# Scores of the second query half: two 64-row tiles with half of the keys each, three products in place of four

## The chip, the core and the metric

The kernel runs on one core of one Trainium2 chip. The metric is the device time of one execution in microseconds (us). Engines are named as in the profile: PE is TensorE (matrix products), PEld its weight loads, DVE is VectorE, ACT is ScalarE, POOL is GpSimd, SP is SyncE, which issues the DMA transfers.

## What is computed

One layer over 1024 tokens with a model width of 1024, in float32: an input projection, two kinds of attention with 8 heads of 64 columns each, an output projection, a sandwich norm and a gated per-layer embedding. The change concerns the scores z of both attentions:

```python
def stick_breaking_attention(q, k, v):          # "SB", strictly causal
    z = jnp.einsum('bqhd,bkhd->bhqk', q_blk, k).astype(jnp.float32) * scale
    past = key_idx[None, :] < t_idx[:, None]
    log_fail = jnp.where(past, jax.nn.log_sigmoid(-z), 0.0)
    suffix = lax.cumsum(log_fail, axis=3, reverse=True) - log_fail
    w = jnp.where(past, jnp.exp(jax.nn.log_sigmoid(z) + suffix), 0.0)

def latent_attention(q_nope, q_rope, k_nope, k_rope, v):   # "MLA"
    z = (jnp.einsum('bqhd,bkhd->bhqk', qn, k_nope)
         + jnp.einsum('bqhr,bkr->bhqk', qr, k_rope)).astype(jnp.float32) * scale
    visible = key_chunk[None, :] <= q_chunk[:, None]       # chunks of 64 tokens
    w = jax.nn.softmax(jnp.where(visible, z, -jnp.inf), axis=-1)
```

In SB and in the first MLA term 64 rows are contracted, in the rotary term (`qr`) 32.

## The kernel before

Every float32 operand of a product is split into a high part and a low part (type float32r), whose sum is the value, and stored so. A product of two values is then up to four products of parts: high x high, high x low, low x high, low x low.

**Units.** Attention goes by units (head c, e; query half s): `SEQ` (line 60) lists the order of the pairs of heads, c below 4 for SB and from 4 on for MLA, e for the head in the pair, s = 0 or 1 for the first or second 512 queries. A unit has four query blocks of 128 (`qi`); block qi of half s sees nk = (4s + qi + 1) x 128 keys. So in the second half nk is 640, 768, 896 or 1024, handled as two parts of h = 320, 384, 448 or 512 keys (`score_tiles`, line 1255), the first half of the keys and the second, each in a PSUM bank of its own.

**Scores.** `load_head` (line 1227) stacks the operands of a unit on all 128 partitions. The key tile `kk` has the 64 rows of a head twice, high and low in alternation; `qa` has the query rows as (high, low), `qb` as (low, high), read from `q_d` forwards and backwards. Two products of 128 contracted rows, qa x kk and qb x kk, so make all four products of parts. `sb_rows` (line 1263) issues them for each part of the keys, and for the part with the diagonal a bf16 product `eye` x `mask` that puts -1e30 on what isn't past; ScalarE then takes two sigmoids from the bank. `mla_rows` (line 1295) has a third product, the rotary one: `qr` x `krs`, 128 rows too (32 rows x high and low of each side). VectorE sets the hidden corner to -1e30, takes the maximum, and ScalarE the exponential. That is 4 products per block of the second half in SB, 6 in MLA. After that come transposes of the weights and the products with the values (`av`, line 1325).

**Order.** Nothing is issued as written. A recorder (lines 340 to 760, `R`) collects all instructions with their operands, estimates a duration for each (`cost`), and `schedule` lays them out engine by engine in a simulation of its own. Each takes its turn by its place in the program, moved by the table `SHIFT` (line 70), which has two numbers for each piece of the program; `FLIP` has the numbers of instructions that change between VectorE and GpSimd or ScalarE. Scores go out 52 places early (`AHEAD`). Other work (projections, gates, norms) is woven in between by `Weaver`, so score products stand among products of other parts. All instructions are issued from one line, 730, so the profile is read by tiles: `t` and `a` are PSUM banks (5 and 3 of them), `u` and `f` buffers in SBUF, `h` larger ones. Loads of a unit are issued a unit ahead (`prepare`).

Of the kernel before, what the change touches and what calls it, by code (L numbers as in the profile page):

```python
# [15 lines left out]
BF16 = mybir.dt.bfloat16  # L16
# [19 lines left out]
MAGIC = 12582912.0  # L36
PI_LO = 3.1415925
# [10 lines left out]
def f(ap):  # L48
# [284 lines left out]
class Recorder:  # L333
# [116 lines left out]
    def columns(self, op, args):  # L450

        return self.elems(args[0]) * (2 if op == "transpose" else 1 if args[1].dtype in (F32R, BF16) else 4)

    @staticmethod
    def elems(ap):
        n = 1
# [4 lines left out]
    def cost(self, eng, op, args, kw, outs, aps, spaces):  # L461
        n = max(self.elems(a) for a in aps)
        ps = any(k == "psum" for _, k in spaces)
        if eng == "PE":
            n = self.elems(outs[0])
            if op == "transpose":
                return 109.0
# [1320 lines left out]
```

## Time and profile before

| | |
|---|---|
| three runs | 773.84, 775.03, 775.43 us |
| the profiled execution | 774.4 us, its span 772.6 us |
| share of the span: DMA queue q1 | 57.4% of 16 engines |
| loads of q_d, k_d in units, issue to landing | 4.7 us (256 KB), 5.3 us (512 KB) |
| table loads on ACT | 18 of 1.28 us |

The page has busy times by engine, the chain of work that ended last, and groups of instructions (operation, output <- inputs, shapes, count, busy us, mean ns of one, idle before). A matmul's end is modelled and overlaps with the next one's start, so the distance from start to start is what a product costs, not its duration. The slices of the page (40 of 19.3 us each) show TensorE's clock and VectorE:

```profile
DVE  5876334499867877788888899999899998888996
...
PEclk9999999999999999999999999999999999999999
```

TensorE has its full clock throughout; VectorE is busiest in the second half of the span.

### The profile page before, as it was taken

The numbers are of one execution on the slowest core, as the hardware profiler recorded it, in microseconds if no ns is written. First come the engines' busy times: TensorE is split into PE (matmuls) and PEld (weight loads), VectorE is DVE, ScalarE is ACT, GpSimd is POOL, SyncE is SP. The second block draws the span as 40 slices with busy tenths as digits, with TensorE's granted clock in tenths as the row PEclk, the third lists the DMA queues.
The fourth block names the chain that finished last, engine by engine and source line by source line (L and its number), as shares of the span: only waits on it lengthen the run. The fifth ranks groups of instructions, "written<-read, shape, count | busy, mean of one in ns | idle before, by whom it ended". The sixth has DMA issues, their size and how long they took to land.

```text
span 772.6 us, 11778 instructions
## 1 busy us (share of the span) xinstructions
PE 754.5 (98%) x3912; PEld 621.5 (80%) x3912; DVE 624.1 (81%) x1184; ACT 384.9 (50%) x898; POOL 346.6 (45%) x315
## 2 busy tenths in 40 slices
PE   6999999999999999999999899999999999999997
PEld 4887889878788878888788788888888888778886
DVE  5876334499867877788888899999899998888996
ACT  6315123333443586565646768776776642433211
POOL 4445111102312258878884712342275114468664
PEclk9999999999999999999999999999999999999999
DMA  9644460269995844566356588686734475172242
GB/s 329 201 171 139 145 213 5 77 218 354 330 341 190 275 155 143 167 206 189 110 184 225 187 290 260 216 302 223 240 116 154 166 254 178 60 268 87 94 150 82
DMA packets 101966, 148.69 MB, mean 192 GB/s; under 512 B 7441, under 2 KB 55057, under 8 KB 101906
## 3 DMA queue, kind: packets, MB, share of 16 engines
q1 hardware_dynamic: 101906, 147.95, 57.4%
q8 instruction: 31, 0.51, 0.3%
q14 instruction: 29, 0.24, 0.1%
HBM read 101.26 MB, written 46.66 MB: 191 GB/s over the span
## 4 chain that ended last, share of the span: by engine, by line
PE 84%; DVE 7%; DMA 4%; ACT 2%; issue 1%; POOL 1%; SPq 1%; POOLq 0%; ACTq 0%; DVEq 0%
PE a L730 58%; PE t L730 26%; DVE u L730 4%; DVE f L730 2%; ACT u L730 1%; DMA u<-k_d 1%; DMA u<-in_w_ple_gate_dram 1%; DMA u<-q_d 1%; DMA u<-in_x_dram 1%; DMA f<-in_positions_dram 1%; DMA q_d<-f 1%; SPq L730 1%; DVE nm L730 1%; ACT f L730 0%; POOL u L730 0%
## 5 line engine op out<-in xcount | busy, mean ns | idle before, releaser
L730 POOL TENSOR_TENSOR u<-u,u 128x512 f32<-128x512 f32 (+16 forms) x134 | 200.5, 1512 | 153.3 <-DVE u L730 64.0
L730 PE MATMUL a<-h,f 128*128 128x512 f32 x864 | 242.1, 405 | 0.0
L730 PEld LDWEIGHTS a<-h,f 128*128 128x128 f32 x864 | 155.2, 189 | 26.8 <-DVE f L730 0.6
L730 DVE TENSOR_TENSOR u<-t,u 128x512 fp32r<-128x512 f32 (+4 forms) x284 | 150.6, 556 | 13.7 <-ACT u L730 10.0
L730 PE MATMUL t<-u,u 128*128 128x512 f32 (+4 forms) x580 | 154.4, 370 | 1.9 <-DMA u<-q_d 0.5
L730 PE MATMUL a<-u,u 128*128 128x512 f32 (+2 forms) x524 | 136.7, 371 | 0.5 <-DVE u L730 0.5
L730 PE MATMUL t<-ident,u 128*128 128x128 f32 x792 | 125.8, 276 | 2.4 <-DVE u L730 2.4
L730 ACT ACTIVATE u<-t 128x512 f32<-128x512 f32 (+5 forms) x208 | 91.0, 509 | 67.7 <-PE t L730 57.8
L730 PEld LDWEIGHTS t<-u,u 128*128 128x128 f32 x580 | 103.4, 189 | 23.2 <-DVE u L730 4.3
L730 ACT CAST u<-t 128x512 fp32r<-128x512 f32 (+3 forms) x187 | 85.6, 495 | 71.0 <-PE t L730 35.3
L730 PE MATMUL a<-h,u 128*128 128x512 f32 (+1 forms) x492 | 118.3, 390 | 0.4 <-DVE u L730 0.4
L730 PEld LDWEIGHTS t<-ident,u 128*128 128x128 f32 x792 | 97.8, 142 | 24.9 <-DVE u L730 7.0
L730 PEld LDWEIGHTS a<-h,u 128*128 128x128 f32 x492 | 90.0, 188 | 21.3 <-issue 1.0
L730 PEld LDWEIGHTS a<-u,u 128*128 128x128 f32 x524 | 93.1, 188 | 17.2 <-DVE u L730 2.2
L730 ACT ACTIVATE u<-t,nms 128x384 f32<-128x384 f32 (+4 forms) x96 | 55.3, 581 | 42.3 <-DVE nms L730 35.3
L730 DVE TENSOR_TENSOR_SCAN u<-u 128x64 f32<-128x64 f32 (+6 forms) x64 | 59.1, 934 | 20.6 <-ACT u L730 20.4
L730 DVE TENSOR_TENSOR u<-u,u 128x512 f32<-128x512 f32 (+13 forms) x91 | 73.2, 820 | 2.0 <-ACT u L730 1.1
L730 DVE TENSOR_TENSOR u<-a,u 64x512 f32<-64x512 f32 (+4 forms) x75 | 47.8, 649 | 15.6 <-ACT u L730 9.7
L730 DVE TENSOR_REDUCE nm<-t 128x1 f32<-128x384 f32 (+4 forms) x96 | 51.6, 545 | 2.1 <-PE t L730 1.3
L730 POOL TENSOR_TENSOR rs<-ms,nhalf 128x8 f32<-128x8 f32 x16 | 27.7, 1731 | 57.0 <-DVE ms L730 37.5
L730 ACT ACTIVATE f<-a 128x512 bf16<-128x512 f32 (+3 forms) x64 | 34.3, 538 | 36.7 <-PE a L730 32.1
L730 PE MATMUL a<-u,h 128*128 128x512 f32 x192 | 49.8, 406 | 0.0
(110 smaller groups left out, 795.5 us busy)
## 6 DMA issues: line engine op xcount, KB each, us to landing
u<-q_d SPq DMA_DIRECT2D x64, 256.0 KB, 4.7
u<-k_d SPq DMA_DIRECT2D x16, 512.0 KB, 5.3
u<-v_d SPq DMA_DIRECT2D x16, 512.0 KB, 4.5
u<-in_w_ple_gate_dram SPq DMA_DIRECT2D x16, 512.0 KB, 5.4
f<-in_w_in_dram SPq DMA_DIRECT2D x14, 512.0 KB, 5.0
v_d<-u SPq DMA_DIRECT2D x12, 512.0 KB, 4.1
f<-in_x_dram SPq DMA_DIRECT2D x9, 512.0 KB, 4.6
k_d<-u SPq DMA_DIRECT2D x9, 512.0 KB, 3.9
```

The source lines that it names most:

```text
L730: x["fn"](*[place(a) for a in x["args"]], **{k: place(a) for k, a in x["kw"].items()})
```

## The change

The first query half (s = 0) keeps two stacked products, with another layout of the keys. In the second half (s = 1) a product contracts 64 rows instead of 128: a 64-row tile on partitions 0 to 63 and another on 64 to 127. Both hold the same queries; the lower has the keys of all even chunks of 64, the upper those of all odd chunks, so each tile has h = nk / 2 keys and writes a bank of its own. Per tile there are three products for SB and for the first term of MLA (`PARTS`: high x high, high x low, low x high; low x low is left out), and two for the rotary term, whose 64 rows are 32 rows of queries with high and low, against the high and the low keys. A block so has 3 pairs of products in SB and 5 in MLA. The diagonal mask becomes a pair too: `step` (64 rows each) x `diag` on the last 64 columns of both banks.

The keys are stored by halves (even chunks, odd chunks) for that; what is read from the banks goes back to its place in the row through a pattern of runs of 64. The planner counts an upper product at 5 ns, gets other costs for bf16 products and waits on DMA, and takes two engines that read one bank as one after the other; `SHIFT` and `FLIP` have other numbers throughout (left out below, as are the planner's lines on banks).

```diff
+PARTS = ((0, 0), (0, 1), (1, 0))
 def columns(self, op, args):
+        if self.upper(args[1]):
+            return 0
+    def upper(self, ap):
+        return ap.shape[0] == 64 and int(ap.offset) >= 64 * self.tiles[ap.tensor.name]["width"]
 def cost(self, eng, op, args, kw, outs, aps, spaces):
+            if self.upper(args[1]):
+                return 5.0
...
-                return n * 0.305
+                return n * 0.416
 LAT:
-("SP", "PE"): 650.0,
+("SP", "PE"): 950.0,
...
+    step, diag = const([128, 128], "step", BF16), const([128, 64], "diag", BF16)
-    k_d = [dram([128, 2, S], f"k_d{i}") for i in range(8)]
+    k_d = [dram([128, 2, 2, S // 2], f"k_d{i}") for i in range(8)]
+    def by_half(ap):
+        return ap.rearrange("q (b a d) -> q a b d", a=2, d=64)
+    def k_evac(dst):
+        def evac(ps, n):
+            t = k4((128, 2, 2, 4, 64), name="qkhl")
+            split(t[:, 0], t[:, 1], by_half(ps), heng=ACT)
+            SP.dma_start(dst[:, :, :, 256 * n:256 * n + 256], f(t.rearrange("q a h b d -> q a h (b d)")))
 def load_head(i, s):
+        if s == 0:
...
+            t = k2((128, 2, 256), name="stk")
+            SP.dma_start(f(t), k_d[c][rows, :, :, 0:256].rearrange("q a h n -> (q a) h n"))
+        else:
+            t = k4((128, 2, 512), name="stq")
+            src = q_d[c][rows, :, half[1]]
+            SP.dma_start(f(t), bass.AP(tensor=src.tensor, offset=src.offset, ap=[[0, 2], *src.ap]))
+            st.append(t)
+            t = k4((128, 2, 512), name="stk")
+            SP.dma_start(f(t), k_d[c][rows].rearrange("q a h n -> h q a n"))
...
+    def scores(s, qi, terms, masked):
+        nk = (4 * s + qi + 1) * 128
+        qc = slice(qi * 128, (qi + 1) * 128)
+        R.bias = -AHEAD
+        if s == 0:
+            ps, w = ps_s(), max(nk, 256)
+            for j, (q, k) in enumerate(terms):
+                mm(ps[:, 0:w], q[:, qc], in_order(k)[:, 0:w // 128], start=(j == 0), stop=(j == len(terms) - 1))
+                if masked and j == 0:
+                    mm(ps[:, nk - 128:nk], eye, mask, start=False, stop=False)
+            return nk, [(ps[:, 0:nk], lambda t: t[:, 0:nk])]
+        h = nk // 2
+        pss = [ps_s() for _ in range(2)]
+        for j, (q, k) in enumerate(terms):
+            for a, ps in enumerate(pss):
+                p = slice(64 * a, 64 * a + 64)
+                mm(ps[:, 0:h], q[p, qc], k[p, 0:h], start=(j == 0), stop=(j == len(terms) - 1),
+                   **({} if a or j else dict(along=pss[1])))
+            if masked and j == 0:
+                for a, ps in enumerate(pss):
+                    p = slice(64 * a, 64 * a + 64)
+                    mm(ps[:, h - 64:h], step[p], diag[p], start=False, stop=False)
+        see = lambda a: lambda t: by_half(t[:, 0:nk])[:, a]
+        return nk, [(ps[:, 0:h], see(a)) for a, ps in enumerate(pss)]
 def sb_rows(i, s, rows):
-            tiles, w = score_tiles(nk)
...
-                mm(ps[:, 0:w], qa[:, qc], kk[:, kw], start=True, stop=False)
-                if ks.stop == nk:
-                    mm(ps[:, h - 128:h], eye, mask, start=False, stop=False)
-                mm(ps[:, 0:w], qb[:, qc], kk[:, kw], start=False, stop=True)
+            nk, tiles = scores(s, qi, terms, True)
 def mla_rows(i, s, rows, es, e):
+            terms = [(st[0][:, a], st[1][:, b]) for a, b in PARTS] + [(st[2], krs[:, b]) for b in range(2)]
-                mm(ps[:, 0:w], qa[:, qc], kk[:, kw], start=True, stop=False)
-                mm(ps[:, 0:w], qb[:, qc], kk[:, kw], start=False, stop=False)
-                mm(ps[:, 0:w], qr[:, qc], krs[:, kw], start=False, stop=True)
+            nk, tiles = scores(s, qi, terms, False)
```

What that does to the order, in rows (output <- moving operand, stationary operand; the numbers name buffers). First TensorE at the first block of the first SB unit of the second half, before. `u_2510` holds the keys, `u_1709` and `u_1949` are qa and qb, `t_184` and `t_157` the two banks:

```order
L730 MATMUL t_184<-u_2510,u_1709 128x320
L730 MATMUL t_184<-u_2510,u_1949 128x320
L730 MATMUL t_157<-u_2510,u_1709 128x320
L730 LDWEIGHTS eye
L730 MATMUL t_157<-mask,eye 128x128
L730 MATMUL t_157<-u_2510,u_1949 128x320
```

The same block after the change; `u_2542` has the keys, `u_2512` the queries, `t_158` is written by the lower tile and `t_225` by the upper:

```order
L748 MATMUL t_158<-u_2542,u_2512 128x320
L748 MATMUL t_225<-u_2542,u_2512 128x320
L748 LDWEIGHTS step
L748 MATMUL t_158<-diag,step 128x64
L748 LDWEIGHTS step
L748 MATMUL t_225<-diag,step 128x64
L748 MATMUL t_158<-u_2542,u_2512 128x320
L748 MATMUL t_225<-u_2542,u_2512 128x320
```

A third pair like the last two rows follows. Four products of full height and one mask have become three pairs of half height and a pair of masks. Pairs stand together in most places, not in all. TensorE at the third block of the next unit after the change (`a_190` is the bank of the value products, of full height):

```order
L748 MATMUL t_218<-u_2739,u_2685 128x448
L748 MATMUL t_291<-u_2739,u_2685 128x448
L748 MATMUL a_190<-u_2074,u_2606 128x512
L748 MATMUL a_190<-u_1881,u_2606 128x512
L748 MATMUL a_190<-u_1905,u_2606 128x512
L748 MATMUL a_190<-u_1024,u_2606 128x512
L748 MATMUL a_190<-u_1853,u_2606 128x512
L748 MATMUL a_190<-u_1917,u_2606 128x512
L748 MATMUL t_218<-u_2739,u_2685 128x448
```

Six full-height products stand between the last product of `t_291` and its partner in `t_218`. In one block of an MLA unit the order has all five products of one tile ahead of the other's (`u_5273` and `u_4377` are the keys and the rotary keys):

```order
L748 MATMUL t_169<-u_5273,u_5268 128x384 x3
L748 MATMUL t_169<-u_4377,u_5261 128x384 x2
L748 MATMUL t_218<-u_5273,u_5268 128x384 x3
L748 MATMUL t_218<-u_4377,u_5261 128x384 x2
L748 MATMUL t_291<-ident,u_5308 128x128
```

Only the two in the middle are neighbours there. Counted over the whole order, the 576 products of half height form 71 stretches with nothing of full height inside.

More of the change, by code (lines that the diff above doesn't have):

```diff
@@ L431, in add @@
                 uses.append(key)
+        if along is not None:
+            self.tiles[along.tensor.name]["users"].append(i)
+            uses.append(along.tensor.name)
         dur = self.cost(eng, op, args, kw, outs, aps, spaces)
         reads = sum(a.shape[-1] > 1 and k == "sbuf" for a, (w, k) in zip(aps[1:], spaces))
+        banks = [a.tensor.name for a, (w, k) in zip(aps[1:], spaces) if k == "psum"]
         port = eng == "POOL" and op != "memset" or eng == "DVE" and (
@@ L513 @@
            ("DVE", "POOL"): 156.0, ("DVE", "SP"): 120.0, ("POOL", "PE"): 180.0, ("POOL", "ACT"): 75.0,
-           ("POOL", "DVE"): 65.0, ("POOL", "POOL"): 102.0, ("POOL", "SP"): 55.0, ("SP", "PE"): 650.0,
-           ("SP", "ACT"): 620.0, ("SP", "DVE"): 620.0, ("SP", "POOL"): 650.0, ("SP", "SP"): 620.0}
+           ("POOL", "DVE"): 65.0, ("POOL", "POOL"): 102.0, ("POOL", "SP"): 55.0, ("SP", "PE"): 950.0,
+           ("SP", "ACT"): 900.0, ("SP", "DVE"): 900.0, ("SP", "POOL"): 950.0, ("SP", "SP"): 900.0}
     def schedule(self):
@@ L553, in schedule @@
         table = None
+        read = {}
         clock = {}
@@ L668, in schedule @@
                     table = x["func"]
+                for key in x["banks"]:
+                    for y, t in read.get(key, {}).items():
+                        if y != e:
+                            s = max(s, t + LAT[y, e])
                 if x["port"]:
@@ L674, in schedule @@
                 free[e] = end
+                for key in x["banks"]:
+                    read.setdefault(key, {})[e] = end
             done += 1
@@ L789, in block_kernel @@
     DVE.tensor_copy(eye, ident)
+    step, diag = const([128, 128], "step", BF16), const([128, 64], "diag", BF16)
+    POOL.memset(step, 1.0)
+    POOL.affine_select(step, step, pattern=[[-1, 128]], compare_op=ALU.is_ge, fill=0.0,
+                       base=0, channel_multiplier=1)
+    DVE.tensor_scalar(diag[0:64], ident[0:64, 0:64], NEG, None, ALU.mult)
+    DVE.tensor_scalar(diag[64:128], ident[64:128, 64:128], NEG, None, ALU.mult)
     ones = const([1, 128], "ones")
@@ L1008, in proj, with q_evac @@
         yield 1.3
-    def qk_evac(dst):
+    def by_half(ap):
+        return ap.rearrange("q (b a d) -> q a b d", a=2, d=64)
+    def q_evac(dst):
         def evac(ps, n):
@@ L1019, in qk_gen @@
         for n in range(2):
-            yield from proj(*wk, n, qk_evac(k_d[c]))
+            yield from proj(*wk, n, k_evac(k_d[c]))
         wq = load_w(C_Q + c * 128, "wq")
         for n in range(2):
-            yield from proj(*wq, n, qk_evac(q_d[c]))
+            yield from proj(*wq, n, q_evac(q_d[c]))
     w0 = {}
     def qk0_gen(n):
-        for k, c0, dst in (("k", C_K, k_d[0]), ("q", C_Q, q_d[0])):
+        for k, c0, evac in (("k", C_K, k_evac(k_d[0])), ("q", C_Q, q_evac(q_d[0]))):
             if k not in w0:
                 w0[k] = load_w(c0, "w" + k)
-            yield from proj(*w0[k], n, qk_evac(dst))
+            yield from proj(*w0[k], n, evac)
     def gate_gen(i):
@@ L1071, in kr_rope @@
         DVE.tensor_tensor(kr[0:32], kr[0:32], tmp[0:32], ALU.add)
-        split(th[0:32], tl[0:32], kr[0:32])
+        for a in range(2):
+            hs = slice(512 * a, 512 * a + 512)
+            split(th[0:32, hs].rearrange("q (b d) -> q b d", d=64), tl[0:32, hs].rearrange("q (b d) -> q b d", d=64),
+                  by_half(kr[0:32])[:, a])
         for rep, src in ((0, th), (1, tl)):
@@ L1151, in lr_qk @@
         for n in range(2):
-            qk_evac(k_d[4 + c])(low_rank([uk[:, 0, cols]], [uk[:, 1, cols]],
+            k_evac(k_d[4 + c])(low_rank([uk[:, 0, cols]], [uk[:, 1, cols]],
                                          [(ckv[0][:, half[n]], ckv[1][:, half[n]])], n), n)
             yield 0.65
-            qk_evac(q_d[4 + c])(low_rank([uqn[0][:, k, cols] for k in range(2)],
+            q_evac(q_d[4 + c])(low_rank([uqn[0][:, k, cols] for k in range(2)],
                                          [uqn[1][:, k, cols] for k in range(2)], lat_q(n), n), n)
@@ L1229, in load_head @@
         rows = slice(64 * e, 64 * e + 64)
-        nk = 512 * (s + 1)
         st = []
-        for src, sl, step in ((q_d[c], half[s], 1), (q_d[c], half[s], -1), (k_d[c], slice(0, nk), 1)):
-            t = k2(name="stq") if len(st) < 2 or s == 0 else k4(name="stk")
-            SP.dma_start(f(t), src[rows, ::step, sl])
+        if s == 0:
+            for src, step in ((q_d[c], 1), (q_d[c], -1)):
+                t = k2(name="stq")
+                SP.dma_start(f(t), src[rows, ::step, half[0]])
+                st.append(t)
+            t = k2((128, 2, 256), name="stk")
+            SP.dma_start(f(t), k_d[c][rows, :, :, 0:256].rearrange("q a h n -> (q a) h n"))
+            st.append(t)
+        else:
+            t = k4((128, 2, 512), name="stq")
+            src = q_d[c][rows, :, half[1]]
+            SP.dma_start(f(t), bass.AP(tensor=src.tensor, offset=src.offset, ap=[[0, 2], *src.ap]))
+            st.append(t)
+            t = k4((128, 2, 512), name="stk")
+            SP.dma_start(f(t), k_d[c][rows].rearrange("q a h n -> h q a n"))
             st.append(t)
@@ L1253, in load_v, with in_order, as_seen @@
         vts[i, s] = v
-    def score_tiles(nk):
-        h = nk if nk <= 512 else nk // 2
-        return [(ps_s(), slice(k, k + h)) for k in range(0, nk, h)], max(h, 256)
+    def in_order(ap):
+        return ap.rearrange("q a (b d) -> q b a d", d=64)
+    def scores(s, qi, terms, masked):
+        nk = (4 * s + qi + 1) * 128
+        qc = slice(qi * 128, (qi + 1) * 128)
+        R.bias = -AHEAD
+        if s == 0:
+            ps, w = ps_s(), max(nk, 256)
[17 more added lines that the diff above has]
+        return nk, [(ps[:, 0:h], see(a)) for a, ps in enumerate(pss)]
+    def as_seen(ps, seen):
+        return ps.rearrange("q (b d) -> q b d", d=64) if len(seen.shape) == 3 else ps
     def row_tile(s, name="row"):
@@ L1317, in mla_rows @@
             row = row_tile(s)
-            for j, (ps, ks) in enumerate(tiles):
-                ACT.activation(row[:, ks], ps[:, 0:ks.stop - ks.start], AF.Exp, bias=nms, scale=MLA_SCALE,
+            for j, (ps, see) in enumerate(tiles):
+                to = see(row)
+                ACT.activation(to, as_seen(ps, to), AF.Exp, bias=nms, scale=MLA_SCALE,
                                accum_out=es[:, 8 * j + 2 * qi + e:8 * j + 2 * qi + e + 1])
```

58 lines of the change are left out of this document (29 added, 29 removed), and 320 rows, old and new, of tables (FLIP, SHIFT).

## The prediction

> **What bounds the kernel now.** I read the page first: the busy times and the chain that ended last.
>
> ```profile
> span 772.6 us, 11778 instructions
> PE 754.5 (98%) x3912; PEld 621.5 (80%) x3912; DVE 624.1 (81%) x1184; ACT 384.9 (50%) x898; POOL 346.6 (45%) x315
> ...
> PE 84%; DVE 7%; DMA 4%; ACT 2%; issue 1%; POOL 1%; SPq 1%; POOLq 0%; ACTq 0%; DVEq 0%
> ```
>
> TensorE is busy for 98% of the span and is 84% of the chain. "Busy" alone could hide waits, so the list of TensorE's waits comes next (engine, what it waited for, us in total, times, longest), and then the stretch of the program in which the second query half is worked on, by windows.
>
> ```profile
> PE t L730 <- DMA u<-in_norm_pre_g_dram: 6.0, 1, 6.0
> PE t L730 <- DVE u L730: 2.8, 5, 1.2
> PE a L730 <- DVE u L730: 0.9, 2, 0.5
> ...
> PE t L730 <- DMA u<-q_d: 0.5, 1, 0.5
> ...
> PE t L730 <- DMA u<-k_d: 0.3, 1, 0.3
> ```
>
> ```profile
> 290.00:606.00 316.00, 312.77 (x1746) 259.70 (x1746) 278.62 (x524) 211.60 (x501) 176.11 (x154) 1.00 0.61 201
> ```
>
> The one long wait is the 6.0 us at the start, which the change doesn't touch; all other waits of the list together are some 6 us. Between 290 and 606 us (the columns are PE, PEld, DVE, ACT, POOL, clock, DMA share, GB/s) TensorE is busy for 312.77 of 316 us at full clock, VectorE for 278.62. So here every 231 ns taken off TensorE's work is 231 ns off the end, as long as VectorE, at 88%, keeps up. What counts is what TensorE needs per product. The timeline has it as distances between starts (start, us, engine, operation, shape, count); the ends are modelled and overlap.
>
> ```profile
> 311.93 0.28 PE L730 MATMUL a<-u 128*128 128x256 f32 x1
> 312.05 0.28 PE L730 MATMUL a<-u,u 128*128 128x256 f32 x1
> 312.17 2.01 PE L730 MATMUL a<-h,f 128*128 128x512 f32 x8
> 314.02 0.27 PE L730 MATMUL t<-ident,u 128*128 128x128 f32 x1
> ```
>
> ```profile
> 314.02 0.49 PE L730 MATMUL t<-ident,u 128*128 128x128 f32 x3
> ...
> 314.58 0.34 PE L730 MATMUL t<-u,u 128*128 128x384 f32 x1
> 314.76 0.60 PE L730 MATMUL t<-ident,u 128*128 128x128 f32 x4
> 315.20 0.22 PE L730 MATMUL t<-mask,eye 128*128 128x128 bf16 x1
> 315.23 0.43 PE L730 MATMUL t<-u,u 128*128 128x384 f32 x1
> 315.49 0.39 PE L730 MATMUL a<-u,u 128*128 128x512 f32 x1
> ```
>
> Eight products of 512 columns start within 314.02 - 312.17 = 1.85 us: 231 ns each, or 0.452 ns per column. One of 256 columns takes 0.12 us and one of 384 takes 0.18 us, so the rate holds for narrower ones (145 ns for 320, 173 for 384, 202 for 448). Each of these has a weight load of 128 columns of its own, and even at 0.12 us the load is hidden. Transposes follow each other by (0.49 - 0.27) / 2 = 0.11 us. A mask product with the 384 columns behind it takes 315.49 - 315.20 = 0.29 us, so the mask costs about 0.12 us.
>
> **The change part by part.** *Fewer streams.* For each query block of the second half the old kernel streams, per half of the keys, two products for stick-breaking (SB) and three for latent attention (MLA): 4 and 6 streams of h = 320, 384, 448 or 512 columns. These rows count them:
>
> ```profile
> L730 PE MATMUL t<-u,u 128*128 128x448 f32 x80 | 22.9, 382 | 0.0
> ...
> L730 PE MATMUL t<-u,u 128*128 128x320 f32 x80 | 17.1, 321 | 0.0
> ...
> L730 PE MATMUL t<-mask,eye 128*128 128x128 bf16 x64 | 14.7, 229 | 0.0
> ```
>
> 80 of each width are 8 heads x 4 + 8 heads x 6. If the two 64-row tiles of a pair stream at the same time, the new kernel has 8 x 3 + 8 x 5 = 64 pair streams of each width. That takes off 16 streams x (320 + 384 + 448 + 512) columns = 26,624 columns x 0.452 ns = **12.0 us**.
>
> *Pairs that are pulled apart.* In the new order eleven score pairs don't stand next to their partner, because 128-row work lies between or one tile's five products all come first: one pair of 512 columns, four of 448, four of 384, two of 320. Each costs a whole further stream: 231 + 4 x 202 + 4 x 173 + 2 x 145 ns = **2.0 us** given back.
>
> *Masks.* 32 of the 64 mask products become pairs of 64 columns, each half with a load of its own. What a mask costs (0.12 us) is far more than its 128 columns (0.06 us at 0.452 ns): what follows it has to load weights that a short product can't hide. That stays, so I take no change. Bounds: 64 columns fewer, -32 x 0.03 = -0.9 us; a second mask not beside the first, +32 x 0.12 = +3.8 us.
>
> *Going into and out of 64-row tiles.* The 512 score and 64 mask products of half height stand in 71 stretches between work of full height: 142 changes of shape that weren't there. No row of the trace has a 64-row product. The nearest change of shape is a transpose that uses 64 columns of the array:
>
> ```profile
> 133.03 0.27 PE L730 MATMUL t<-ident,f 128*128 128x128 f32 x1
> 133.06 0.44 PE L730 MATMUL a<-f,h 128*128 128x416 f32 x1
> 133.34 0.27 PE L730 MATMUL t<-ident,f 128*64 128x128 f32 x1
> 133.36 0.81 PE L730 MATMUL a<-f,h 128*128 128x416 f32 x3
> 134.01 0.27 PE L730 MATMUL t<-ident,f 128*128 128x128 f32 x1
> ```
>
> A full transpose and a product of 416 columns take 0.31 us (133.03 to 133.34). The 64-column transpose and three such products take 0.67 us, and 0.11 + 3 x 0.19 = 0.68: the change of shape costs nothing there. The upper end is a pipeline that runs empty each time, at most a product's modelled duration less its spacing:
>
> ```profile
> L730 PE MATMUL a<-h,f 128*128 128x512 f32 x864 | 242.1, 405 | 0.0
> ```
>
> 405 - 231 = 174 ns, or 142 x 174 ns = 24.7 us. A gain is excluded, since a boundary takes no work away. Between 0 and 24.7 us I stay near the row that changes shape, with 15 ns a boundary: **2.1 us**.
>
> The Trainium skill speaks against this choice: "TensorEngine Tiling (Array Packing)", Tiling Modes, Key Properties, says that a change of tiling mode, unlike a change of tile, drains TensorE. By that rule the sum would go toward the upper end just worked out, an estimate of some 789 us; the 64-column row doesn't bear it out, but no row here changes the row tiling.
>
> *Weight loads.* A pair needs two loads where a product needed one. With both tiles loading side by side that is 0.11 us, under the shortest stream (0.145), and costs nothing; one after the other it is 0.22 us, which is the first rival.
>
> *Loads and layouts.* The keys lie by halves now, so their transfers come in runs half as long; the two query loads of a second-half unit become one. TensorE's waits for k_d and q_d are 0.8 us in total, and loads are issued a unit ahead; if that cover went, I'd expect a few times these 0.8 us. Key operands of the first half are streamed in runs of 64 columns. No row shows TensorE doing that. VectorE shows it: values read from alternate runs of 64 in a bank (u<-a) against values read in order (u<-t):
>
> ```profile
> L730 DVE CAST u<-t 128x256 fp32r<-128x256 f32 x13 | 5.4, 415 | 10.2 <-PE t L730 9.6 <-PE a L730 0.6
> ...
> L730 DVE CAST u<-a 128x256 fp32r<-128x256 f32 x5 | 1.9, 418 | 2.7 <-PE a L730 2.7
> ```
>
> 418 against 415 ns: I take zero for such patterns on every engine.
>
> *Planner.* The tables and three cost rules are new, so everything moves a little. VectorE has 1130 rows in place of 1159 and GpSimd 330 in place of 309, mostly multiplications of 512 columns that change sides; ScalarE has 741 in place of 726. These engines have room (81, 45 and 50%). All of TensorE's waits after the start are some 6 us, so a new order can win or lose about 3; I take zero.
>
> Sum: -12.0 + 2.0 + 0 + 2.1 = -7.9 us on the profiled run's 774.4 us (the span of 772.6 and 1.8 around it) = 766.5. The median shown, 775.03, is 0.6 above that run, so on it the sum gives 767.1. **I predict 767 us.**
>
> **The rivals.** *One weight load at a time (R1).* The two loads of a pair share one path: 0.22 us per pair. With 512 columns (0.231) it is hidden; with 320, 384 and 448 a pair takes 75, 47 and 18 ns more, 0.14 us in all. The first pair of a set loads under the work ahead of it, so SB has two such pairs a block and MLA four: 8 x (2 + 4) x 0.14 = 6.7 us, and 3.8 us for the masks. 767.1 + 10.5 = 777.6 at worst, 774 with the masks unharmed. For it: transposes go at one load per 0.11 us, the load's own pace. Against it: the tiles use different partitions, so nothing forces them to share.
>
> The Trainium skill has both halves of this: "TensorE: Matmul & The Clock Gate", section LDWEIGHTS, says that a load's time goes by its columns and not its rows, so half a tile loads no faster; Part 3 of that page says that loads of different row groups overlap. The 0.11 us of the trace's transposes fits the first (its figure gives an estimate of 107 ns for 128 columns), and no row can show the second.
>
> *Each change of tiling empties the pipeline (R2, slower).* Its place is the 142 boundaries, its price up to 174 ns each: 767.1 - 2.1 + 24.7 = 789.7 us. It decides from (12.0 - 2.0) / 142 = 70 ns a boundary. For it: a full-height product has partial sums in all 128 rows when the 64-row tiles want to start. Against it: the 64-column transpose above.
>
> *The tiles don't run side by side (R3: the change doesn't do what it says).* Then the second half takes 8 x 6 + 8 x 10 = 128 streams of each width in place of 80: 48 x 1664 x 0.452 ns = 36.1 us more, 811 us. No row of the trace has products of two tiles, which speaks neither way.
>
> *VectorE becomes the bound (R4).* Its 278.6 us would stand against 304 us in the middle stretch, 92%, and less with the multiplications moved away; it could eat 3 us, 770. That lies within my forecast.
>
> **How the numbers follow.** Forecast with its neighbours, 760 to 771 (new order 3 us better or worse, boundaries from 0 to 40 ns): 0.53. R1 or boundaries of 40 to 80 ns, 771 to 778: 0.25. R2, 778 to 791: 0.14. R3: 0.06. Better than 760: 0.02. A measurement of this kernel can tell about 0.2% from no change, 773.5 to 776.6 us. Of the 0.25, 0.10 lies below that, 0.08 within and 0.07 above. So faster 0.53 + 0.02 + 0.10 = 0.65, same 0.08, slower 0.07 + 0.14 + 0.06 = 0.27. The range 760 to 784 leaves out R3, the upper part of R2 and the 0.02 below: 0.17.
>
> **What would show it.** In the new profile the two products of a pair should start within some 10 to 20 ns of each other, and pairs follow by 145 to 231 ns. Spacings of 0.22 us whatever the width mean R1, single starts a whole stream apart R3, a gap of over 70 ns where a stretch of half-height products begins or ends R2. Weight loads should rise from 3912 by about 220, and TensorE's busy time fall by some 8 us. The prediction is wrong if TensorE's waits grow by several us, since then the new order and not the tiles sets the time.

## The result, and the profile after

The changed kernel takes 1050.15 us (median of 4 runs, 1049.8 to 1051.97) against 775.11 us (773.84 to 775.43): 1.356 times as long, 95% interval 1.3534 to 1.3581. The prediction said 767 us, in a range from 760 to 784. It was wrong by more than any of its rivals allowed for.

The page of the profile after, the same lines as before (the profiled execution took 1051.97 us):

```profile
span 1050.3 us, 12201 instructions
PE 813.7 (77%) x4136; PEld 639.6 (61%) x4136; DVE 623.1 (59%) x1158; ACT 392.5 (37%) x914; POOL 366.0 (35%) x333
...
PE   6999999999976954995962149638473856999997
...
PEclk9999999999988977896995578878685977999999
DMA  9435318896435322434522235423133133754233
...
PE 55%; DMA 25%; issue 7%; DVE 5%; ACT 3%; SPq 3%; POOL 2%; POOLq 0%; DVEq 0%; ACTq 0%
```

No engine has much more work, but all stand idle for long between slices 12 and 34, which is where the second query half is. DMA has 25% of the chain in place of 4%, and in the same slices the 16 DMA engines are *less* busy than before. TensorE's clock is down to 5 to 9 tenths there, so its own work also takes longer: 813.7 us of busy time in place of 754.5 (773.7 in e1 below, which has the same products at nearly full clock). The stretch that the prediction rested on, by windows (the columns are PE, PEld, DVE, ACT, POOL, clock, DMA share, GB/s), and TensorE's waits:

```profile
290.00:606.00 316.00, 206.45 (x1059) 154.37 (x1057) 158.45 (x256) 120.21 (x275) 120.43 (x105) 0.80 0.35 114
```

```profile
PE a L748 <- DVE u L748: 64.8, 5, 23.3
PE t L748 <- DMA u<-k_d: 29.5, 4, 14.1
PE t L748 <- DMA u<-q_d: 28.8, 2, 27.9
PE t L748 <- DVE u L748: 23.6, 9, 19.3
```

The waits for k_d and q_d were 0.8 us together; they are 58.3 us now, and those for VectorE's buffers `u` are 88.4 in place of 3.7. Behind some of these stand loads too: the page's group of GpSimd's multiplications, with its idle time ahead, waits for gate_d.

```profile
L748 POOL TENSOR_TENSOR u<-u,u 128x512 f32<-128x512 f32 (+17 forms) x151 | 219.8, 1470 | 240.3 <-DMA u<-gate_d 103.3
```

What the queue that issues the loads does shows why. SyncE's timeline (start, us, issue), and the windows of its long rows:

```profile
540.89 8.93 SPq L748 DMA_DIRECT2D u<-q_d  x1
549.92 10.36 SPq L748 DMA_DIRECT2D ple_d<-f  x1
560.38 0.71 SPq L748 DMA_DIRECT2D u<-v_d  x1
561.14 6.28 SPq L748 DMA_DIRECT2D u<-q_d  x1
567.52 6.65 SPq L748 DMA_DIRECT2D u<-k_d  x1
574.22 10.31 SPq L748 DMA_DIRECT2D u<-qr_d  x1
584.59 5.19 SPq L748 DMA_DIRECT2D u<-gate_d  x1
589.88 0.57 SPq L748 DMA_DIRECT2D u<-v_d  x1
```

```profile
541.00:550.00 9.00, 0.73 (x4) 0.25 (x2) 2.04 (x7) 1.26 (x4) 1.80 (x2) 0.81 0.13 49
550.00:560.00 10.00, 0.00 (x0) 0.00 (x0) 0.00 (x0) 0.00 (x0) 0.00 (x0) 0.50 0.13 50
```

Before, the same issues took less:

```profile
320.57 1.18 SPq L730 DMA_DIRECT2D u<-q_d  x2
321.85 0.55 SPq L730 DMA_DIRECT2D u<-v_d  x1
322.49 0.45 SPq L730 DMA_DIRECT2D u<-k_d  x1
```

From 550 to 560 us no engine does anything, and the DMA share is 0.13: 2 of 16 engines, 50 GB/s. A transfer of 512 KB at 50 GB/s takes 10.5 us, which is about the length of the longest rows. While one such transfer runs, SyncE's queue stands, even where the next issue (a store of ple_d) has nothing to do with it.

What these transfers have in common stands in the diff. 41 loads of the second half are written with a dimension of 2 outermost on the DRAM side: `[[0, 2], *src.ap]` for q_d (16) and for the rotary queries (8), `"q a h n -> h q a n"` for k_d (16), and one of the rotary keys. In the kernel before each of these loads begins with 64 rows or more. The Trainium skill has this as a rule, in "DMA: Bandwidth & Descriptors", Rules for kernel authors: an outermost dimension of fewer than 16, such as a leading broadcast, confines a transfer to that many DMA engines. The 0.13 and the 50 GB/s agree with it.

### The profile page after: what moved, and what is told of

The parts are those of the page before. It is cut to its first block, busy times and chain, and to the rows that moved or that the text cites. A ratio compares the mean times of both kernels' runs of the same rounds, so it can differ in the third digit from the quotient of the medians.

```text
span 1050.3 us, 12201 instructions
## 1 busy us (share of the span) xinstructions
PE 813.7 (77%) x4136; PEld 639.6 (61%) x4136; DVE 623.1 (59%) x1158; ACT 392.5 (37%) x914; POOL 366.0 (35%) x333
## 4 chain that ended last, share of the span: by engine, by line
PE 55%; DMA 25%; issue 7%; DVE 5%; ACT 3%; SPq 3%; POOL 2%; POOLq 0%; DVEq 0%; ACTq 0%
PE a L748 39%; PE t L748 17%; DMA u<-gate_d 7%; DMA u<-k_d 5%; DVE u L748 4%; DMA u<-q_d 3%; SPq L748 3%; DMA f<-in_w_out_dram 2%; ACT u L748 2%; DMA y_d<-u 2%; POOL u L748 2%; DMA k_d<-f 1%; DMA ple_d<-f 1%; DMA gate_d<-f 1%; DVE f L748 1%
## 5 line engine op out<-in xcount | busy, mean ns | idle before, releaser
L748 POOL TENSOR_TENSOR u<-u,u 128x512 f32<-128x512 f32 (+17 forms) x151 | 219.8, 1470 | 240.3 <-DMA u<-gate_d 103.3
L748 PE MATMUL t<-u,u 64*128 64x512 f32 (+6 forms) x752 | 154.0, 421 | 116.3 <-DMA u<-k_d 29.5
L748 PEld LDWEIGHTS t<-u,u 64*128 64x128 f32 (+1 forms) x752 | 99.0, 213 | 152.4 <-issue 80.5
L748 PE MATMUL t<-ident,u 128*128 128x128 f32 x792 | 135.0, 287 | 13.6 <-POOL u L748 8.8
L748 DVE TENSOR_TENSOR u<-u,u 128x512 f32<-128x512 f32 (+9 forms) x68 | 74.8, 1110 | 90.8 <-ACT u L748 61.4
L748 DVE TENSOR_REDUCE nm<-t 128x1 f32<-128x384 f32 (+5 forms) x96 | 52.4, 550 | 74.5 <-PE t L748 73.8
L748 DVE TENSOR_TENSOR_SCAN u<-u 128x448 f32<-128x448 f32 (+5 forms) x64 | 62.7, 987 | 27.8 <-ACT u L748 26.8
L748 ACT ACTIVATE u<-t,nms 128x384 f32<-128x384 f32 (+5 forms) x96 | 55.2, 582 | 38.4 <-DVE nms L748 37.7
L748 ACT CAST u<-u 128x512 fp32r<-128x512 f32 (+1 forms) x31 | 19.7, 635 | 131.1 <-POOL u L748 100.4
L748 ACT ACTIVATE f<-a 128x512 bf16<-128x512 f32 (+2 forms) x64 | 34.2, 536 | 88.3 <-PE a L748 80.5
L748 POOL TENSOR_TENSOR u<-u 128x512 f32<-128x512 f32 (+7 forms) x33 | 36.6, 1113 | 74.3 <-DMA u<-gate_d 32.7
L748 POOL MEMSET u<- 128x128 f32 x64 | 12.1, 204 | 131.9 <-PE t L748 71.5
```

The source lines that it names most:

```text
L748: x["fn"](*[place(a) for a in x["args"]], **{k: place(a) for k, a in x["kw"].items()})
```

## The experiments

In the expectations a letter is the name of a theory within that text. Times are medians of device time; where the text says so, a single run.

**The loads.** e1 is the changed kernel with each of the 41 transfers issued as two of 64 partitions, which then begin with 64 rows. Order, products and layout stay as they are. e2 does it for the 16 query loads alone.

```diff
+ args = [place(a) for a in x["args"]]
+ if x["eng"] == "SP" and int(args[1].ap[0][1]) == 2 and args[0].shape[0] == 128:
+     dst, src = args
+     for a in range(2):
+         x["fn"](dst[64 * a:64 * a + 64], bass.AP(tensor=src.tensor,
+                 offset=src.offset + a * int(src.ap[0][0]), ap=src.ap[1:]))
+     continue
...
```

> The changed kernel with its 41 transfers whose source pattern begins with a dimension of 2 (16 query, 16 key, 8 rotary query and 1 rotary key load) issued as two transfers of 64 partitions each; everything else as in the changed kernel. Theory A (such a transfer is served by 2 of the 16 DMA engines, and the queue stands behind it): the long waits of TensorE go, the time falls from 1050 us to between 762 and 780 us, SyncE's issues take 0.5 us again, and TensorE's clock is full. Theory B (the new order of instructions starves TensorE, whatever the transfers): it stays above 1000 us. Theory C (64-row products hold TensorE up): it stays above 1000 us too, with waits that end in nothing but TensorE's own work. Within A, the sum of the prediction says 767, a boundary cost of 85 to 90 ns (as the spacings of the changed kernel's trace suggest) says 774 to 778.

> As before, but only the 16 query loads of the second half are split; the 16 key loads, 8 rotary query loads and 1 rotary key load keep the pattern that begins with 2. Theory A: a transfer of 256 packets of 2 KB takes 256 x 84 ns / 2 = 10.8 us on two engines, so 16 of the 41 slow transfers (172 of some 400 us) go and about 0.4 to 0.5 of the loss of 275 us with them: 900 to 950 us. Theory B or C: no change from 1050.

Measured: e1 806.95 us, ratio 1.0416 (1.0398 to 1.0433); e2 932.45 us in a single run. So 243.2 of the 275.0 us go with the leading 2: 117.7 us with the 16 query loads (7.4 us each), 125.5 us with the other 25 (5.0 us each). That e1 stays above the 762 to 780 us that theory A gave says that the loads aren't the whole loss. TensorE's waits in e1:

```profile
PE a L754 <- DVE u L754: 6.5, 3, 5.1
PE t L754 <- DMA u<-in_norm_pre_g_dram: 6.1, 1, 6.1
PE t L754 <- DVE u L754: 4.3, 7, 0.9
PE t L754 <- ACT u L754: 3.9, 6, 1.1
PE t L754 <- DMA u<-q_d: 1.2, 2, 1.0
```

The wait for k_d is gone, the one for q_d is 1.2 us. The other direction: the kernel before with its second-half loads written part by part, so that 32 of them (forward queries and keys) begin with 2 (e3; the 16 backward ones are split), and the same with all 48 split (e4). There is no product of half height and no new layout in either.

```diff
- SP.dma_start(f(t), src[rows, ::step, sl])
+ s_ = src[rows, ::step, sl]
+ SP.dma_start(f(t), s_.rearrange("q a n -> a q n") if s else s_)
```

> The kernel before, with 128-row products and its own order, but the rows of q and k of the second-half units stacked as (part, row) in place of (row, part), so that 32 of its loads have a source pattern that begins with 2 (16 key loads of 128 packets of 4 KB, 16 query loads of 128 packets of 2 KB; the other 16 query loads are issued in two parts). Theory A: two packets at a time, 10.2 and 5.4 us for a transfer, SyncE's queue stands, and the time grows by 100 to 250 us with no 64-row product in it. Theories B and C: 775 us, as before.

> As e3, with those 48 loads of the second half all issued as two transfers of 64 partitions each. Theory A: 775 us as before, within 3 us: the stacking by part costs nothing, nor do 48 more issues. If it were the stacking itself (other rows next to each other in memory), it would stay as slow as e3.

Measured, a single run each: e3 926.08 us, e4 774.51. The leading 2 by itself costs the kernel before 151 us, 4.7 us for each of 32 transfers (before: 4.7 and 5.3 us from issue to landing). In e3's list of waits, behind the two largest (for ACT's and VectorE's buffers `u`), the loads stand where they hardly stood before:

```profile
PE t L736 <- DMA u<-k_d: 21.5, 5, 7.6
PE t L736 <- DMA u<-gate_d: 16.1, 1, 16.1
```

**The steps between full and half height.** e1 is still 32 us slower than before, though it streams less. Its timeline at one stretch of half height:

```profile
365.41 1.19 PE L754 MATMUL a<-h,f 128*128 128x512 f32 x4
366.53 0.50 PE L754 MATMUL t<-u,u 64*128 64x512 f32 x2
366.87 0.20 PE L754 MATMUL t<-diag,step 64*128 64x64 bf16 x2
366.91 0.71 PE L754 MATMUL t<-u,u 64*128 64x512 f32 x4
367.56 0.97 PE L754 MATMUL a<-h,f 128*128 128x512 f32 x3
```

Two products of a pair do run at the same time: four of 512 columns lie within 367.56 - 366.91 = 0.65 us, which is less than three streams one after the other. But a step costs time. The last of the four full products, and the weight loads of the first pair:

```profile
366.21 0.39 PE L754 MATMUL a<-h,f 128*128 128x512 f32 x1
...
366.53 0.19 PEld L754 LDWEIGHTS t<-u,u 64*128 64x128 f32 x2 [0.36 <-issue]
```

The pair starts 366.53 - 366.21 = 0.32 us after the product ahead, where 0.23 is the pitch: TensorE starts nothing for 0.09 us longer. Its weight loads start with it and not under the product ahead, and the next product comes 366.87 - 366.53 = 0.34 us later, again 0.11 us more than the pitch: the load stands by itself. On the way out it is the same. Over the steps in e1's trace the first part is mostly 85 to 100 ns in both directions (median 94), the second has medians of 108 ns in and 103 ns out.

e5 puts the pairs that had been pulled apart together again. e6 takes e1 and moves a product of full height ahead of the third pair of a block wherever nothing forbids it, which makes 102 stretches in place of 71, so 62 more steps. e7 lets the planner know 195 ns for each step and plan anew.

```diff
 # e6, where the order is issued: c is of full height, a and b are the third pair
+ if half(a) and half(b) and up(a) != up(b) and not half(c) and k > 3 and half(pes[k - 3]) and half(pes[k - 4]):
...
+         before[a] = c
 # e7, in schedule
+ m = self.ins[i]["op"] == "matmul" and self.ins[i]["args"][1].shape[0] == 64
+ if m != mode:
+     d += 195.0
+     mode = m
```

> e1_all_split with pairs that the order had pulled apart brought together where that is possible: the two products of a pair follow each other at once, 68 stretches of half height in place of 71, and 1.4 us less of unpaired streams. Theory D (each step between full and half height costs some 0.195 us: TensorE runs empty, 0.085 to 0.09, and the next weights load unhidden, 0.11): -1.4 - 6 x 0.195 = -2.6 us, 804. Theory F (the new order's waits, not the tiles, are what is left of the loss): no change beyond 1 us.

> e1_all_split with the last pair of 31 stretches moved behind the full-height product that follows it, so the same products stand in 102 stretches in place of 71: 62 more steps between full and half height, and nothing else. Theory D: +62 x 0.195 = +12.1 us, 819. Theory E (a half-height pair is slower in itself, wherever it stands): no change. Theory F: no change, or a few us either way.

> e1_all_split with one more rule in the planner: a product of another height than the one before it takes 195 ns longer. The order is planned again; it has 74 stretches. TensorE's waits after the start were 18.4 us in e1_all_split and 6 us in the kernel before. Theory D with the waits coming from a plan that doesn't know the steps: waits fall by 5 to 12 us, and the time with them, to 796 to 803 (3 more stretches cost 1.2). If the waits come from the new tables: 807 as before, within 4.

Measured: e5 803.45 (802.59 to 804.54), e6 815.84 (815.33 to 817.27), e7 817.99 (814.6 to 821.5). e5 is 3.5 us faster than e1, but TensorE is busy for only 1.3 us less (772.4 us); most of it is shorter waits. e6 takes 8.9 us more than e1, 0.14 us for each further step. TensorE's busy time in e1 and then in e6:

```profile
PE 773.7 (96%) x4136; PEld 611.8 (76%) x4136; DVE 631.1 (78%) x1158; ACT 391.8 (49%) x914; POOL 368.4 (46%) x333
```

```profile
PE 785.8 (97%) x4136; PEld 613.5 (75%) x4136; DVE 629.1 (77%) x1158; ACT 391.6 (48%) x914; POOL 368.3 (45%) x333
```

It grows by 12.1 us, 0.195 us a step, which is what the timeline says. TensorE's waits after the start fall from 18.4 to 14.9 us in exchange: part of the steps' cost went into time that had been waiting. e7 was a miss: an order planned with a price for the step was 11 us *worse*. That was the first sign that a new plan can lose time by itself.

e9 therefore does the whole change without a product of half height: layout, banks and a mask on each bank as changed, but with full-height products of stacked operands (four in SB, six in MLA) and full-height masks, planned anew. Its loads stack the rows as before, so none begins with a 2.

> The whole change (layout of the keys, tables, planner's costs, masks on both banks) with full-height products in the second half: two products of 128 rows per bank for both attentions and a third for the rotary term, as in the kernel before, in place of the three and five pairs; loads stack the rows as before and none begins with a dimension of 2; the places of the products left out are not issued. TensorE's sum against e1_all_split: the steps go, -27.7 us, the unpaired streams, -2.0, the saved streams come back, +12.0, and 32 full-height masks are added, +3.8: -13.9 us. Theory D: 793 us, or down to 781 where the waits that the steps made go too. Theory F: the time stays at 805 to 820, with waits of 15 us and more. Theory E: 12 to 20 us below e1_all_split like D, so that e6 decides between them.

Measured: 805.58 (802.68 to 808.17). It has no step and is no faster than e1, which speaks against the steps as the whole of it; but its order isn't e1's either. e10 takes the order out of the question: the planner gets e1's durations, so that VectorE, ScalarE and GpSimd have e1's order instruction by instruction (in both traces they do), and each product stands where its pair stood (`part` 1 is planned at the 5 ns of an upper product; what is skipped is planned and not issued).

```diff
- mm(ps[:, 0:h], q[p, qc], k[p, 0:h], start=(j == 0), stop=(j == len(terms) - 1),
+ q_, k_ = (stq[:, j, qc], stk[:, a, 0:h]) if j < 3 and j != 2 else (terms[3][0][:, qc], krx[:, a, 0:h]) if j == 3 else (q[:, qc], k[:, 0:h])
+ mm(ps[:, 0:h], q_, k_, start=(j == 0), stop=(j == (1 if masked else 3)), skip=(j in (2, 4)), part=a,
...
+ if part == 1:
+     dur = 5.0
```

> e1's own order (every instruction of VectorE, ScalarE and GpSimd stands where it stood, and each product too), but each pair of half-height products of the second query half is one full-height product per half of the keys, with the stacked operands of before: four in place of six in SB, six in place of ten in MLA. So no step between full and half height is left (142 in e1). Distances from start to start without waiting add up to 761.0 us in e1; this order without the half-height products should come to 746 (before: 745.6). Theory S (each step costs about 0.195 us, and that is part of what e1 lost; the rest is waiting that this order brings): e1's 807 less 15 = 792 us, between 787 and 797. Theory O (the order alone keeps TensorE waiting, steps don't matter): 803 to 808, with the time that is saved gone into waits. Theory F (steps free, half-height products only cheaper): 818 to 822.

Measured: 787.7 us (786.61 to 790.54), ratio 1.0158 (1.0136 to 1.0181). In one and the same order the half-height products cost 19.3 us *more* than the full-height ones that they replace, though they stream 12 us less. e10 at the place shown for e1:

```profile
363.15 1.09 PE L766 MATMUL a<-h,f 128*128 128x512 f32 x4
364.07 0.62 PE L766 MATMUL t<-u,u 128*128 128x512 f32 x2
364.54 0.23 PE L766 MATMUL t<-mask,eye 128*128 128x64 bf16 x2
364.60 0.70 PE L766 MATMUL t<-u,u 128*128 128x512 f32 x2
365.14 0.86 PE L766 MATMUL a<-h,f 128*128 128x512 f32 x3
```

From the first full product to the first one after the stretch it is 365.14 - 363.15 = 1.99 us, with four streams in the block. In e1 it was 367.56 - 365.41 = 2.15 us with three: 0.16 us more for 0.23 us less streaming, so 0.39 us for the two steps. Over the whole program, the distances from start to start of all products without a wait ahead add up to 761.0 us in e1 and 747.7 in e10. With the 12.0 us of streams that is 25.3 us for 142 steps; without the 2.0 us that e1's pulled-apart pairs give back, which are no steps, it is 23.3: **0.16 to 0.18 us a step**. The rest of the 19.3 us is mostly shorter waits (18.4 us after the start in e1, 14.5 in e10).

**The rest.** e10 is 11.8 us above before and has neither slow loads nor steps. e11 has e9's products and layout, with `SHIFT`, `FLIP` and planner constants of before (instructions that the change adds aren't counted, so each number meets the instruction it was made for). e12 is the same with the half-height pairs, e13 the same as e11 with a block's products bank by bank as before. e14 is the kernel before with one edit, the products term by term over both banks as the change has them; e15 the kernel before with one edit too, the change's planner constants.

```diff
 # e14
- mm(ps[:, 0:w], qa[:, qc], kk[:, kw], start=True, stop=False)
...
- mm(ps[:, 0:w], qb[:, qc], kk[:, kw], start=False, stop=True)
+ for q in (qa, qb):
+     for ps, ks in tiles:
+         h = ks.stop - ks.start
+         mm(ps[:, 0:w], q[:, qc], kk[:, ks.start:ks.start + w], start=(q is qa), stop=(q is qb))
...
 # e15
- return n * 0.305
+ return n * 0.416
- ("SP", "PE"): 650.0,
+ ("SP", "PE"): 950.0,
...
```

> The change's layout of the keys by halves, its extra masks and its scores in a bank per half, but full-height products (none of half height), and the order by the numbers of before: SHIFT, FLIP and the planner's constants of before, with the instructions that the change adds left uncounted, so that each number falls on the instruction that it was made for. Theory T (what e1 and the kernel with full-height products lose in waits lies in the change's own table and planner constants): 775 + 3.8 for 32 masks, so 776 to 785 us. Theory L (the layout by halves itself, with its runs of 64 and its reads back to place, costs the time): 795 to 806.

> The whole change with its 41 transfers split as in e1, its half-height pairs and masks, but in the order that the numbers and planner constants of before give; 84 stretches of half-height products, so 168 steps. Theory S with T (a step costs 0.143 to 0.195 us, the table costs the rest): the kernel with this layout and full-height products (776 to 785) + 168 x 0.143 to 0.195 = 24 to 33, less 12 for the streams: 788 to 806, most likely 796. Theory L: 807 or more. If steps cost nothing: 764 to 775, faster than before.

> As the kernel with the change's layout, full-height products and the numbers of before (815), but the products of a block stand bank by bank as before (all of the first half of the keys, then all of the second), not term by term over both banks. Theory K (products term by term finish both banks at the end of the block, so ScalarE and VectorE get the first bank late and the banks stay taken): 776 to 786. Theory L (the layout by halves costs the time): 805 to 816. Theory N (any change of the program lets the hand-made numbers fit worse): anything from 785 to 815.

> The kernel before with one edit: the score products of a block of the second half stand term by term over both banks, as the change has them, not bank by bank. Layout, loads, masks and numbers are those of before. Theory K: 785 to 815. Theory L: 775 to 778. Theory N: 780 to 800.

> The kernel before with the change's planner constants alone (0.416 in place of 0.305 ns per column of a bf16 product, 900 to 950 in place of 620 to 650 ns of waiting on a DMA); its instructions are the same, the order is planned anew. Theory N: 780 to 800. Otherwise 774 to 777.

| | us | ratio to before |
|---|---|---|
| e11, layout, full height | 815.37 (814.37 to 816.31) | 1.0511 (1.0493 to 1.0528) |
| e12, the same with pairs | 835.35 (835.11 to 838.16) | 1.0775 (1.0755 to 1.0795) |
| e13, e11 bank by bank | 796.93 (796.68 to 799.04) | 1.0304 (1.0285 to 1.0324) |
| e14, before, term by term | 790.88 (789.3 to 795.0) | 1.0226 (1.0195 to 1.0256) |
| e15, before, other constants | 801.81 (801.33 to 802.88) | 1.0361 (1.0345 to 1.0376) |

e12 against e11 would be 0.19 us a step (20.0 us and the 12.0 us of streams, for 168 steps) if their orders were the same; in the traces the instructions of VectorE, ScalarE and GpSimd stand in different orders in the two, so it is no proof of its own. e11 refutes that before's numbers would bring its time back. The telling one is e15: its instructions are those of before, and a plan made with other constants alone costs 27.5 us. Its page and its waits:

```profile
PE 763.0 (95%) x3912; PEld 622.5 (78%) x3912; DVE 636.8 (80%) x1184; ACT 384.7 (48%) x898; POOL 348.2 (44%) x315
```

```profile
PE t L730 <- DVE u L730: 7.2, 11, 1.5
PE a L730 <- DVE u L730: 6.4, 4, 3.6
PE t L730 <- DMA u<-in_norm_pre_g_dram: 5.9, 1, 5.9
PE a L730 <- ACT f L730: 2.1, 3, 1.7
```

The waits for VectorE are 13.6 us where they were 3.7. In this kernel `SHIFT` moves 980 pieces of the program, each by numbers of its own, and whatever moves the planner's clock makes another order: +16.5 (e14), +22.6 (e13), +27.5 (e15), +39 us (e11). Only e15 is a new plan and nothing else. e14 fits theory K as well as N: term by term costs 16.5 us there and 18.4 us between e13 and e11, so that finishing both banks late may have a price of its own. As a new plan alone costs 27.5 us, these runs can't tell. With its own numbers the change's order does well among these: 11.8 us (e10).

## Why the prediction was wrong, point by point

**Loads and layouts: the step that failed.** It took zero, and "a few times these 0.8 us" if the cover went. The cover did go, and the price was 243.2 us. The step looked at run lengths and at the waits of before; it didn't look at the order of the dimensions in each new transfer, though the `[[0, 2], *src.ap]` stands in the diff. No rival had it. Nor did the step ask what stands behind a slow transfer in SyncE's queue, which is every other load. The prediction's sign of being wrong, TensorE's waits growing by several us, did appear (12 us in all before, 230 after), but the reason it gave, the new order, accounts for little of that: e1 has the same order and 24.5 us of waits. Without this step the forecast would still have missed, since e1's 807 us lies above its range, by the steps and the plan below.

The layout in runs of 64 by itself costs ScalarE next to nothing, as taken: its group of 512 columns and its sigmoids of 448, in e11 and then in the kernel before:

```profile
L774 ACT ACTIVATE u<-t 128x512 f32<-128x512 f32 x64 | 35.1, 611 | 22.4 <-PE t L774 21.3 <-ACT u L774 0.9 <-POOL u L774 0.2
L774 ACT ACTIVATE u<-t 128x448 f32<-128x448 f32 x32 | 15.0, 557 | 10.6 <-PE t L774 10.5
```

```profile
L730 ACT ACTIVATE u<-t 128x512 f32<-128x512 f32 x64 | 35.4, 612 | 21.9 <-PE t L730 17.3 <-issue 3.3 <-POOL u L730 1.2
L730 ACT ACTIVATE u<-t 128x448 f32<-128x448 f32 x32 | 15.3, 552 | 6.7 <-PE t L730 6.7
```

611 against 612 ns and 557 against 552. TensorE has as little of it: in e11's trace products of the first half whose key operands lie in runs of 64 follow each other at 118, 178 and 234 ns for 256, 384 and 512 columns (medians), those of before at 118, 175 and 232.

**Going into and out of 64-row tiles: mis-sized.** It took 15 ns a boundary, 2.1 us, from a change of *columns* in the trace. Measured: 0.16 to 0.18 us against full-height products in the same order (e10), 0.195 of busy time and 0.14 of the whole time from added steps (e6), so 23 to 28 us in 142 steps. Rival R2 had the sign and half of the mechanism. Its upper end of 174 ns is about what a step costs, but by luck: the pipeline that runs empty is only some 94 ns of it, and the rest is something that R2 left out, that the weights of the first product aren't loaded under the last product of the other shape. The Trainium skill ("TensorEngine Tiling (Array Packing)", Key Properties) states that a change of tiling mode drains TensorE; the 85 to 100 ns in which nothing starts agree with it. The 64-column row didn't speak for row tiling.

**Fewer streams: right.** In e1's trace 249 of the 288 pairs start within 10 ns of each other, and within a stretch pairs follow at 147, 175, 200 and 228 ns for 320, 384, 448 and 512 columns (medians), where single products of before follow at 146, 175, 204 and 232. So the 12.0 us are really saved, and R3 is refuted. **Weight loads: right**, R1 is refuted: it asked for 0.22 us a pair whatever the width.

**Pairs pulled apart:** not measured by itself. e5 undoes 1.4 of the 2.0 us and six steps; TensorE's busy time falls by 1.3 us, where its expectation had 2.6.

**Masks: about as taken.** In the stretch shown a pair of masks costs 0.14 us (367.56 - 366.87 = 0.69, less two streams of 0.23 and the 0.09 of the step), where 0.12 was taken. No run isolates the term.

**Planner: mis-sized.** It took zero and 3 us either way. e10, where little else is left, is 11.8 us above before: without waits its products come to 747.7 us in place of 745.6, and TensorE's waits after the start to 14.5 us in place of 6. That these waits are all the order's wasn't shown by a kernel that has the new layout in exactly before's order: the layout's part and that of the products term by term stay open. The sigmoids and products above don't point to the layout. (The pages count 26 instructions fewer on VectorE, 18 more on GpSimd and 16 more on ScalarE; the prediction had 29, 21 and 15.)

**VectorE as the bound (R4)** doesn't decide. In e10, with neither slow loads nor steps, it is busy for 282.36 of the 316 us of the middle stretch (278.62 before), and TensorE for 308.10:

```profile
290.00:606.00 316.00, 308.10 (x1717) 253.24 (x1715) 282.36 (x498) 207.52 (x486) 174.59 (x149) 0.99 0.60 201
```

Each term is the difference from one run to the next, so they add up by construction: 243.2 (loads) + 19.3 (half height, net of the streams) + 11.8 (what e10 keeps) = 274.3 of 275.0 us, with before at 775.11 to 775.94 us on the chips of these runs. A mend exists for the loads alone. With it the change loses 32 us; no version of the change here beats the kernel before.

## What to carry to other kernels

Read the outermost dimension of every new DMA pattern before its run lengths: two transfers of 64 rows each cost nothing here, and one with a 2 in front took 2 of 16 DMA engines and held up the queue behind it. Half-height pairs save one stream a block (0.15 to 0.23 us) and pay two steps a stretch (0.3 to 0.4 us). From these numbers I estimate that they pay off only in stretches of several blocks; no run here has such an order. And in a kernel whose order was fitted to one plan, measure what a new plan alone costs (here 27.5 us, e15) before giving a loss to the change.

## What the runs showed of the hardware

- A transfer on 2 DMA engines (share 0.13 of 16) moves 50 GB/s, and in the rows shown the issue behind one stands for 5 to 10 us, be it a load or a store.
- TensorE's granted clock goes down where it waits long: 0.50 in the ten idle microseconds shown and 0.80 over the stretch of 316 us. Its busy time is 813.7 us in the changed kernel, at a mean clock of 0.88, and 773.7 in e1, which has the same products, at 0.993.
- Two tiles of 64 rows load weights and stream side by side at full rate (pairs of 512 columns every 228 ns, single products every 232). A change between full and half height costs 0.14 to 0.2 us: some 94 ns in which nothing starts, and about 0.11 us of a weight load that isn't hidden.
